# Down-projection of a decoder layer in two seven-product groups of eight blocks instead of one

## The chip, the cores and the metric

The kernel runs as one program on one core of a Trainium2 chip. The metric is the device time of that core in microseconds, the median of several runs of the same program. A separate profiled execution gives the trace; its span runs from the first to the last instruction.

## What is computed

One decoder layer in float32, 1024 tokens by 1024 channels. The change touches its last part only, the feed-forward block with a causal depthwise convolution, and the residual and norm behind it:

```python
def conv_ffn(xn, w_up, conv_w, conv_b, w_down):
    u = xn @ w_up                                  # (1024, 5632)
    c = conv_b + sum(upad[:, j:j + S] * conv_w[j] for j in range(3))
    gate, val = jnp.split(c, 2, axis=-1)
    return (jax.nn.silu(gate) * val) @ w_down      # w_down: (2816, 1024)
...
    x = x + conv_ffn(xn, w_up[l], conv_w[l], conv_b[l], w_down[l])
return rmsnorm(x, norm_final_w)
```

## The kernel before

Everything lies transposed: channels on the 128 partitions, tokens along the free dimension, two halves `hf` of 512 tokens. The hidden activation h has 2816 rows, 22 blocks of 128 (`NF`); the output has 1024 rows, 8 blocks `m`. Each float32 operand is split into two parts of the type fp32r, a high part (a cast on ScalarE, written ACT in the profile) and a low part (source minus high part, a subtraction on VectorE, DVE), and a product of two blocks is three matmuls: high by high, high by low, low by high (`product`, lines 835 to 837, and `mms`, line 996). `split` (lines 755 and 756) and `split_pair` (L110 and L112) and `load_w` (L129 and L131) make the parts for activations and weights.

Where a two by two arrangement of blocks is multiplied by a two by two arrangement, the kernel can form seven products of sums of blocks instead of eight products of blocks. The up-projection (`hidden`) does so for all its blocks. It names the weight blocks A11, A12, A21, A22 and the activation blocks B11, B12, B21, B22, with sums S1 to S4 of weights and T1 to T4 of activations. `sum_pair` makes the sums of weights on GpSimd (POOL, lines 96 to 99), four additions of 512 columns for a pair of outputs.

The last step of `hidden` stores h block by block to DRAM (`hd`); `down` reads it back. `raw_h` loads one half block (256 KB, tile `hr`, nine buffers) on the queue of SyncE (SP), `parts_h` splits it into a tile `h`; those tiles come in turn from two pools, 19 (`HP`) and 9 (`HPB`) of them.

`down` before the change:

- Plain blocks 0 to 5 (`N1 = 6`): 16 pieces, each one output `m` and three blocks, both halves, in `self.pieces`; four outputs at a time (first 4 to 7, then 0 to 3). The result is added to x, which lies in `x3` and is loaded from DRAM in two DMAs of 2 MB. In the course of these pieces the last steps of the convolution are finished (`DEFER`), their results stored (`STORE`), and the splits of the blocks needed next are made (`preps`, `sums`).
- Blocks 6 to 13 as one group of seven products. Rows m and m + 4 of the output form a pair. First a loop over the four pairs does the two products with A11 and A12; then a second loop does the other five products of each pair in turn (S1, S2, S4, S3, A22). The results are added to x on DVE directly from PSUM (lines 1052 to 1072).
- Blocks 14 to 21 plainly: 8 outputs for the first half, then for the second half, 24 matmuls each, with the squares for the last norm behind each. The last two outputs of the second half are done in quarters of 256 tokens, so that the norm (`last_norm`: column sums L158, `rstd_cols` L165 and L167, `spread` L173, scaling L1143, output DMAs L1144) starts earlier.

`next_w` returns the next weights; `ahead` loads and splits them one step before they are used, from two buffers for each of the tiles `wh`, `wl`, `sh` and `sl`, three of `raw` and two of `rv`; with `deep`, the load from DRAM is another step ahead. PSUM has eight banks here, four named `d` and four named `y`.

The order of the instructions on each engine isn't that of the code: a scheduler at build time takes, on each engine, the instruction of the highest priority (normally the first in the code) among those that are ready by its own costs, and a tile whose buffer is still taken isn't ready.

## Time and profile before

| what | value |
|---|---|
| median of 3 runs | 1355.06 us (1354.48 to 1355.87) |
| profiled execution, its own time | 1356.2 us |
| span of the profiled execution | 1354.3 us |
| granted TensorE clock, mean | 0.996 |
| busy in the span | PE 99%, weight loads (PEld) 81%, DVE 75%, ACT 45%, POOL 36% |
| HBM traffic | 129.61 MB read, 48.76 MB written |

In the profile PE is TensorE, SP the queue of SyncE from which the loads are issued. A row of the timeline gives the start in us, the time it took, the engine, the line of the kernel, the operation, the tile written and the tiles read, the shape and the count; in square brackets stands the idle time of the engine ahead of it and who ended it. Times are counted from the start of the span.

### The profile page before, as it was taken

Reading aid. Unit: us, or ns where it says so; the run is one execution under the profiler, and the core shown is the slowest. Engines: PE = TensorE matmul, PEld = TensorE weight load, DVE = VectorE, ACT = ScalarE, POOL = GpSimd, SP = SyncE. Lnnn points to the kernel's source line nnn. Section 1 sums busy time; section 2 is a strip of 40 time slices with the busy share of each in tenths; the row PEclk is TensorE's granted clock in tenths of the full one; section 3 lists DMA queues with packets and bytes.
Section 4 is the critical chain, followed back from the end, with each engine's and each line's share of the span. In section 5 each row is a group of like instructions: output and inputs, shape, how many; then the busy total and the mean of one; then the engine's idle time right before and its main releaser. Section 6 shows DMA issues by size and latency. Waiting matters only on the chain.

```text
span 1354.3 us, 17160 instructions
## 1 busy us (share of the span) xinstructions
PE 1335.0 (99%) x6304; PEld 1103.6 (81%) x6304; DVE 1009.8 (75%) x1454; ACT 603.9 (45%) x942; POOL 483.1 (36%) x350
## 2 busy tenths in 40 slices
PE   7999999999999999999999999999999999999997
PEld 6888888888887777878888888888888888888886
DVE  8846775388898875355689888888888898986454
ACT  8422232376667664334444334433443345433343
POOL 0436651010102125741455565555555611231011
PEclk9999999999999999999999999999999999999999
DMA  6334443966554235334422222122212248651342
GB/s 255 140 113 164 143 156 114 272 174 175 156 133 144 77 116 219 117 119 136 166 82 88 71 91 94 62 79 93 93 63 83 92 141 311 215 177 64 94 134 85
DMA packets 62470, 179.50 MB, mean 133 GB/s; under 512 B 6833, under 2 KB 15153, under 8 KB 62385
## 3 DMA queue, kind: packets, MB, share of 16 engines
q1 hardware_dynamic: 50928, 160.98, 36.7%
q10 hardware_dynamic: 11456, 17.41, 3.5%
q8 instruction: 50, 0.82, 0.2%
q14 instruction: 36, 0.29, 0.1%
HBM read 129.61 MB, written 48.76 MB: 132 GB/s over the span
## 4 chain that ended last, share of the span: by engine, by line
PE 62%; DVE 17%; POOL 7%; issue 7%; DMA 4%; ACT 3%; POOLq 0%; DVEq 0%; SPq 0%; ACTq 0%
PE t L836 7%; PE t L837 7%; PE t L835 7%; POOL us L965 3%; PE y L996 3%; PE d L996 3%; PE sc L568 3%; PE g L150 2%; PE g L151 2%; DVE c L958 2%; PE g L152 2%; DVE wl L112 2%; DMA gr<-gd 2%; PE sc L151 2%; PE sc L152 2%
## 5 line engine op out<-in xcount | busy, mean ns | idle before, releaser
L970 ACT ACTIVATE c<-us,vecs 128x1024 f32<-128x1024 f32 x44 | 54.8, 1248 | 163.2 <-POOL us L965 160.0
L965 POOL TENSOR_TENSOR us<-us,rstd 128x1024 f32<-128x1024 f32 x42 | 100.7, 2414 | 52.8 <-DVE wl L131 34.3
L110 ACT CAST sh<-sf 128x1024 fp32r<-128x1024 f32 x62 | 64.9, 1051 | 106.2 <-POOL sf L97 61.8
L129 ACT CAST wh<-raw 128x1024 fp32r<-128x1024 f32 (+2 forms) x60 | 60.7, 1012 | 104.8 <-PE sc L151 33.1
L971 DVE SCALAR_TENSOR_TENSOR c<-us,vecs,c 128x1024 f32<-128x1024 f32 x44 | 67.1, 1527 | 51.9 <-ACT c L970 51.9
L131 DVE TENSOR_TENSOR wl<-raw,wh 128x1024 fp32r<-128x1024 f32 (+2 forms) x60 | 75.3, 1256 | 39.1 <-ACT wh L129 29.3
L96 POOL TENSOR_TENSOR sf<-rv 128x512 f32<-128x512 f32 x30 | 42.5, 1417 | 166.7 <-DMA rv<-in_w_up 73.2
L112 DVE TENSOR_TENSOR sl<-sf,sh 128x1024 fp32r<-128x1024 f32 x62 | 88.3, 1426 | 8.2 <-ACT sh L110 8.2
L167 POOL TENSOR_TENSOR rs<-ms,mhalf 128x8 f32<-128x8 f32 (+2 forms) x9 | 14.5, 1614 | 159.1 <-DVE ms L165 148.5
L150 PE MATMUL g<-xh,wh 128*128 128x512 f32 x176 | 70.7, 402 | 0.1
L152 PE MATMUL g<-xh,wl 128*128 128x512 f32 x176 | 70.4, 400 | 0.0
L151 PE MATMUL g<-xl,wh 128*128 128x512 f32 x176 | 70.4, 400 | 0.0
L98 POOL TENSOR_TENSOR sf<-raw,rv 128x512 f32<-128x512 f32 x30 | 41.6, 1386 | 59.9 <-DVE sl L112 59.9
L572 DVE CUSTOM_DVE_ANT_0 L<-sc,bias 128x128 f32<-128x128 f32 (+7 forms) x64 | 47.7, 752 | 17.4 <-PE sc L568 14.1
L551 POOL MEMSET aT<- 128x128 f32 x32 | 6.1, 204 | 152.0 <-PE t L597 101.6
L573 ACT ACTIVATE L<-L,sm 128x128 f32<-128x128 f32 (+7 forms) x64 | 49.6, 778 | 20.7 <-DVE sm L572 18.2
L97 POOL TENSOR_TENSOR sf<-sf,raw 128x512 f32<-128x512 f32 x31 | 58.0, 1870 | 1.6
L972 DVE SCALAR_TENSOR_TENSOR c<-us,vecs,c 128x1024 f32<-128x1024 f32 x44 | 56.2, 1279 | 0.6
L725 POOL TENSOR_TENSOR gr<-gr,rstd 128x1024 f32<-128x1024 f32 x16 | 39.4, 2467 | 41.4 <-DMA gr<-gd 41.2
L112 DVE TENSOR_TENSOR wl<-raw,wh 128x1024 fp32r<-128x1024 f32 (+1 forms) x35 | 52.8, 1508 | 0.1
L151 PE MATMUL sc<-ml,wh 128*128 128x512 f32 x128 | 50.1, 391 | 0.6 <-DVE ml L746 0.6
L568 PE MATMUL sc<-u,u 128*128 128x512 f32 (+2 forms) x192 | 49.8, 359 | 0.1
(444 smaller groups left out, 4351.4 us busy)
## 6 DMA issues: line engine op xcount, KB each, us to landing
u<-qd SPq DMA_DIRECT2D x72, 256.0 KB, 6.1
raw<-in_w_down SPq DMA_DIRECT2D x27, 512.0 KB, 3.7
raw<-in_w_in SPq DMA_DIRECT2D x25, 512.0 KB, 4.4
hr<-hd SPq DMA_DIRECT2D x50, 256.0 KB, 5.3
raw<-in_w_up SPq DMA_DIRECT2D x23, 512.0 KB, 3.6
hd<-c SPq DMA_DIRECT2D x22, 512.0 KB, 2.8
rv<-in_w_up SPq DMA_DIRECT2D x21, 512.0 KB, 3.5
gr<-gd SPq DMA_DIRECT2D x16, 512.0 KB, 3.6
```

The source lines that it names most:

```text
L112: nc.vector.tensor_tensor(lo, src, hi.bitcast(F32), ALU.subtract)
L131: self.lo = (eng or nc.vector).tensor_tensor(wl, raw, wh.bitcast(F32), ALU.subtract)
L150: nc.tensor.matmul(ps, wh[:, kc + o, :], ah, start=first and n == 0, stop=False)
L151: nc.tensor.matmul(ps, wh[:, kc + o, :], al, start=False, stop=False)
L152: nc.tensor.matmul(ps, wl[:, kc + o, :], ah, start=False, stop=last and n == len(kcs) - 1)
L568: nc.tensor.matmul(sc[:, lo + n0:lo + n1], qs, k[c][part][:, n0:n1], start=part == 0, stop=part == 1)
L835: nc.tensor.matmul(ps, ah[:, k, :], bh, start=first and n == 0, stop=False, skip_group_check=skip)
L836: nc.tensor.matmul(ps, ah[:, k, :], bl, start=False, stop=False, skip_group_check=skip)
L837: nc.tensor.matmul(ps, al[:, k, :], bh, start=False, stop=last and n == len(ks) - 1, skip_group_check=skip)
L965: i = (nc.vector if m % NF == 0 else nc.gpsimd).tensor_tensor(us[:, 2:], us[:, 2:], self.rstd, ALU.mult)
L971: nc.vector.scalar_tensor_tensor(c, us[:, 1:T + 1], cw[1], c, ALU.mult, ALU.add)
L996: nc.tensor.matmul(ps, v[:, n, :], x, start=n == i == 0, stop=n == len(js) - 1 and i == 2)
```

## The change

The plain blocks at the front are three (`N1 = 3`), then come two groups of eight blocks (`NS = 8`) in seven products, then three plain blocks. Each group runs in three loops over the four output pairs: first A11 and A12; then S1, S2 and, one pair later, S4; then S3 and, one pair later, A22. Products of one pair are accumulated in the same PSUM bank and added to x in between: S4 upon S1, S2 upon the A11 product, S3 upon that, A22 upon that. So each of the seven products is followed by one addition of its bank to x, seven for a pair, where before there were nine.

The sums of weights are no longer made four at a time from one load: for the second loop (`"p2"`) the pair is loaded and three additions on POOL give S1, S2 and S4; for the third (`"p3"`) half of it is loaded again and one subtraction gives S3. Differences of h are made in two units, `sums_h2` (T1, T2 and the split of B22; one subtraction on POOL and one on DVE) and `sums_h3` (T3 and T4; two on POOL and one on DVE), where before `sums_h` made five on DVE; the halves of h are loaded for both. All preparations are one list `units`, of which each step takes a written number (`ready`). x is loaded in four DMAs of 1 MB. The weights of the last three blocks are split once and kept in h tiles (`last_w`), where before they were loaded twice. `HPB` is 7, `STORE` (1, 7), `DEFER` (2, 5).

```diff
-HP, HPB, HR = 19, 9, 9
-STORE = (1,9)
-DEFER = (4,8)
-N1 = 6
+HP, HPB, HR = 19, 7, 9
+STORE = (1, 7)
+DEFER = (2, 5)
+N1, NS = 3, 8
...
+    def sums_w(self, src, kind):
+        nc = self.nc
+        tt = nc.gpsimd.tensor_tensor
+        n = 2 if kind == "p2" else 1
+        g = self.tl(self.wp, [P, n, 4, P], "raw", bufs=RAW)
+        nc.sync.dma_start(g.rearrange("p a k c -> p (a k) c"), src[0][:, :4 * n])
+        v = self.tl(self.uw, [P, 2, 4, P], "rv", bufs=2)
+        nc.sync.dma_start(v.rearrange("p a k c -> p (a k) c"), src[1])
+        if n == 1:
+            tt(v[:, 0], g[:, 0], v[:, 0], ALU.subtract)
+            return (v, ("S3", "A22")), None
+        s = self.tl(self.cpl, [P, 2, 4, P], "c")
+        tt(s[:, 0], v[:, 0], v[:, 1], ALU.add)
+        tt(s[:, 1], s[:, 0], g[:, 0], ALU.subtract)
+        tt(g[:, 1], g[:, 1], s[:, 1], ALU.subtract)
+        return (s, ("S1", "S2")), (g[:, 1:2], ("S4",))
+
+    def split_sums(self, two, one):
+        ops = {}
+        for pool, h, l, part in ((self.uw, "sh", "sl", two), (self.wp, "wh", "wl", one)):
+            if part:
+                src, names = part
+                n = len(names)
+                hi, lo = self.split(*(self.tl(pool, [P, n, 4, P], t, F32R) for t in (h, l)), src)
+                for i, name in enumerate(names):
+                    ops[name] = hi[:, i], lo[:, i]
+        return ops
...
+        self.pieces = [4, 5, 6, 7, 0, 1, 2, 3]
+        src += [(self.w_dn[m:m + 2, :, :N1, :].rearrange("m p k c -> p m k c"), 2 * N1) for m in self.pieces[::2]]
+        for a in (N1, N1 + NS):
+            for kind in ("p1", "p2", "p3"):
+                for m in range(4):
+                    g, v = (self.w_dn[o, :, a:a + NS, :] for o in (m, m + 4))
+                    src.append((g, NS) if kind == "p1" else ((g, v), kind))
...
-    def sums_h(self, k):
-        b11, b12, b22, b21 = (self.raw_h(N1 + j, hf) for j, hf in ((k, 0), (k, 1), (k + 4, 1), (k + 4, 0)))
-        tt = self.nc.vector.tensor_tensor
...
+    def sums_h2(self, a, k):
+        b11, b12, b22 = (self.raw_h(a + j, hf) for j, hf in ((k, 0), (k, 1), (k + 4, 1)))
+        self.nc.gpsimd.tensor_tensor(b11, b12, b11, ALU.subtract)
+        self.nc.vector.tensor_tensor(b12, b22, b11, ALU.subtract)
+        for name, t in (("T1", b11), ("T2", b12), ("B22", b22)):
+            self.B[name, k] = self.parts_h(t)
+
+    def sums_h3(self, a, k):
+        b11, b12, b21, b22 = (self.raw_h(a + j, hf) for j, hf in ((k, 0), (k, 1), (k + 4, 0), (k + 4, 1)))
+        tt = self.nc.gpsimd.tensor_tensor
         tt(b12, b22, b12, ALU.subtract)
+        tt(b21, b21, b11, ALU.subtract)
+        self.nc.vector.tensor_tensor(b21, b21, b12, ALU.subtract)
+        for name, t in (("T3", b12), ("T4", b21)):
+            self.B[name, k] = self.parts_h(t)
...
+            units, self.lw = [], {}
+            for a in (N1, N1 + NS):
+                units += [lambda a=a, k=k, n=n, o=o: self.one_h(n, a, k, k + o, 0) for n, o in (("B11", 0), ("B21", 4)) for k in range(4)]
+                units += [lambda a=a, k=k, f=f: f(a, k) for f in (self.sums_h2, self.sums_h3) for k in range(4)]
+            units += [lambda j=j, hf=hf: self.load_h(j, hf) for hf in range(2) for j in range(N1 + 2 * NS, NF)]
+            units += [lambda m=m: self.last_w(m) for m in range(KC)]
...
+            ready = ((1, 1, 1, 1, 1, 2, 3, 3, 3, 1, 1, 0), (1, 1, 1, 1, 1, 2, 2, 2, 2, 2, 2, 2))
+            for g, counts in enumerate(ready):
+                counts, ys, late = list(counts), [], []
+                for m in range(4):
+                    wh, wl = self.next_w()
+                    y, ps = bank(1), bank(0) if g else pss[m, 0]
+                    ys.append(y)
+                    self.product(y, (wh[:, 0:4], wl[:, 0:4]), "B11", skip=True)
+                    self.product(ps, (wh[:, 4:8], wl[:, 4:8]), "B21", first=g > 0)
+                    for p in (y, ps):
+                        add(m, 0, p)
+                    prepare(counts.pop(0))
+                def p2(m, w, ps):
+                    self.product(ps, w["S4"], "B22", first=False, skip=True)
+                    add(m, 1, ps)
+                def p3(m, w, y):
+                    self.product(y, w["A22"], "T4", first=False, skip=True)
+                    add(m + 4, 0, y)
+                for m, y in enumerate(ys):
+                    w = self.next_w()
+                    ps = bank(0)
+                    self.product(ps, w["S1"], "T1", skip=True)
+                    add(m + 4, 1, ps)
+                    self.product(y, w["S2"], "T2", first=False, skip=True)
+                    add(m, 1, y)
+                    late.append((m, w, ps))
+                    if m:
+                        p2(*late.pop(0))
+                    if m == 3:
+                        p2(*late.pop(0))
+                    prepare(counts.pop(0))
+                for m, y in enumerate(ys):
+                    w = self.next_w()
+                    self.product(y, w["S3"], "T3", first=False, skip=True)
+                    add(m + 4, 1, y)
+                    late.append((m, w, y))
+                    if m:
+                        p3(*late.pop(0))
+                    if m == 3:
+                        p3(*late.pop(0))
+                    prepare(counts.pop(0))
...
-                    w = self.next_w()
+                    w = self.lw[m]
...
-                    mms(ps, w, 1, js, a, b, lambda n, m=m: tail.pop(0)() if a and n == (4 if m < KC - 1 else 2) else None)
+                    mms(ps, w, 1, js, a, b, lambda n, m=m: tail.pop(0)() if a and n == (1 if m < KC - 1 else 0) else None)
```

## The prediction

> **What bounds the kernel now.** I read the page first, for who is busy; then the chain of waits that ended last, for where the end comes from in the stage that changes; then the busy time by windows, for what the helpers have left there; then the timeline, for single durations.

> ```profile
> span 1354.3 us, 17160 instructions
> PE 1335.0 (99%) x6304; PEld 1103.6 (81%) x6304; DVE 1009.8 (75%) x1454; ACT 603.9 (45%) x942; POOL 483.1 (36%) x350
> ```

> PE has work in 99% of the span. So a matmul less is time less, as long as its operands are ready. The chain (columns: start, us, what) shows the stage to be a row of matmuls:

> ```profile
> 1111.23 2.04 PE d L1023 x9
> ...
> 1259.49 5.44 PE y L996 x24
> ...
> 1303.01 0.79 PE d L158 x8
> ...
> 1309.40 0.44 PE d L173 x4
> 1309.84 0.44 PE y L173 x4
> ...
> 1332.08 2.87 PE d L996 x24
> ...
> 1339.63 0.79 PE d L158 x8
> ...
> 1342.67 0.22 PE d L173 x2
> ...
> 1344.94 0.43 DVE x L1083
> ...
> 1345.87 0.84 PE d L158 x6
> ...
> 1346.97 0.70 POOL rs L167
> ```

> The down-projection begins at 1111.23 and its last matmul ends at 1344.94: 233.7 us, with 9.4 us behind it. One matmul of 512 columns costs 5.44 / 24 = 0.2267 us, one of 256 columns 2.87 / 24 = 0.12. What the stage's PE work should take, counted from the code: 288 (six plain blocks: 8 outputs x 2 halves x 6 x 3) + 336 (seven products x 4 pairs x 4 x 3) + 336 (eight plain blocks, less the last two outputs' second half) = 960 of 0.2267, 96 short ones of 0.12, and the sums and spreads (0.79 + 0.88 + 0.79 + 0.44): 217.6 + 11.5 + 2.9 = 232.0. PE stalls are only 1.7 us.

> The windows (busy us of PE, PEld, DVE, ACT, POOL; PE clock; DMA share; GB/s):

> ```profile
> 800.00:900.00 100.00, 99.81 (x437) 81.24 (x436) 86.26 (x84) 37.93 (x41) 57.64 (x43) 1.00 0.24 79
> ...
> 1110.00:1120.00 10.00, 10.00 (x46) 8.29 (x45) 8.50 (x12) 4.40 (x6) 1.62 (x1) 1.00 1.04 401
> ...
> 1150.00:1160.00 10.00, 10.00 (x45) 8.28 (x45) 9.97 (x13) 2.03 (x2) 0.66 (x1) 1.00 0.60 200
> 1160.00:1170.00 10.00, 10.00 (x45) 8.26 (x44) 9.06 (x11) 6.06 (x10) 6.25 (x4) 1.00 0.65 225
> ```

> PE is full in all four; DVE is nearly full too around 1150. DVE, with POOL beside it, is the next limit, and the change hands both more work per matmul.

> **What PE loses.** Plain blocks at the front 3 (144 matmuls), two groups (672), plain blocks at the end 3 (144): 960 instead of 1008. Of these 942 are long and 36 short: 213.6 + 4.3 + 2.9 = 220.8 us, which is 11.2 less than 232.0. This is certain; the question is how many stalls come in.

> **What DVE and POOL gain.** Prices come from these rows (start, us, what):

> ```profile
> 1114.73 0.95 DVE L131 TENSOR_TENSOR wl<-raw,wh 128x768 fp32r<-128x768 f32 x1
> ...
> 1118.53 3.09 DVE L756 TENSOR_TENSOR h<-hr,h 128x512 fp32r<-128x512 f32 x5
> ...
> 1129.97 2.38 POOL L965 TENSOR_TENSOR us<-us,rstd 128x1024 f32<-128x1024 f32 x1 [18.36 <-DVE wl L131]
> ...
> 1163.00 2.99 DVE L756 TENSOR_TENSOR h<-hr,h 128x512 fp32r<-128x512 f32 x3
> 1163.67 1.77 POOL L96 TENSOR_TENSOR c<-sl 128x512 f32<-128x512 f32 x1 [13.01 <-DMA sl<-in_w_down]
> ...
> 1165.92 0.67 DVE L1042 TENSOR_TENSOR x<-x,y 128x512 f32<-128x512 f32 x1
> 1166.51 2.88 DVE L756 TENSOR_TENSOR h<-hr,h 128x512 fp32r<-128x512 f32 x2
> ...
> 1168.92 1.62 POOL L99 TENSOR_TENSOR c<-raw,c 128x512 f32<-128x512 f32 x1
> 1169.96 1.67 DVE L112 TENSOR_TENSOR sl<-c,sh 128x1024 fp32r<-128x1024 f32 x1 [0.57 <-ACT sh L110]
> ...
> 1207.36 1.22 DVE L112 TENSOR_TENSOR sl<-c,sh 128x1024 fp32r<-128x1024 f32 x1
> ...
> 1208.70 1.29 POOL L96 TENSOR_TENSOR c<-raw 128x512 f32<-128x512 f32 x1 [6.62 <-DVE sl L112]
> ```

> Five splits in a row take 3.09, so a 512-column DVE operation costs 0.60, one of 1024 columns 1.20, one of 768 0.87. A POOL addition alone costs 1.29. Together they are dearer: from 1163.00 to 1171.63 DVE does five splits, one addition from PSUM and one split of 1024 columns, 4.8 us by those prices, waits 0.57 for ACT, and needs 8.63: 3.3 us are lost while POOL does four additions (5.2 us alone). Burst price: a POOL microsecond takes 63% of a microsecond from DVE. The addition from PSUM (L1042) took its plain 0.67 in the middle of it; the splits wait.

> [...]

> Stretch I runs from 1118.5, where DVE is done with the stage before, to the third phase of the first group. PE's part: plain blocks end at 1111.2 + 144 x 0.2267 = 1143.9, first phase 96 matmuls (21.8), second 144 (32.6): 1198.3, so 79.8 us. DVE in it: 28 splits of h (16.8) and 8 differences (4.8); weight splits 2 x 0.87 + 4 x 1.2 + 4 x 1.8 + 1.2 = 14.9; the last convolution steps, five operations of 1024 (6.0); 32 additions from PSUM (12 + 8 + 12; 19.2). Sum 61.7, of it 42.5 with both inputs in SBUF. POOL: 4 + 8 differences of h, 12 + 1 sums of weights, 25 x 1.29 = 32.3, and two L965 of 2.38: 37.0. Stretch II, from there to the third phase of the second group (21.8 + 21.8 + 32.6 = 76.2 us): DVE 16.8 + 4.8 + 16.8 + 28 additions (16.8) = 55.2, POOL 28 x 1.29 = 36.1. DVE and POOL together are 124% and 120% of the time. What such a load does to PE is shown by the up-projection before it, groups in 800 to 895.2 us (five steps of 84 matmuls; columns: line, operation, count, busy us, mean ns, idle):

> ```profile
> L971 DVE SCALAR_TENSOR_TENSOR c<-us,vecs,c 128x1024 f32<-128x1024 f32 x10 | 15.0, 1499 | 12.9 <-ACT c L970 12.9
> L112 DVE TENSOR_TENSOR sl<-sf,sh 128x1024 fp32r<-128x1024 f32 x10 | 12.1, 1212 | 0.0
> ...
> L396 DVE TENSOR_TENSOR us<-t,s 128x512 f32<-128x512 f32 x5 | 3.4, 684 | 0.0
> ...
> L112 DVE TENSOR_TENSOR wl<-rv,wh 128x512 fp32r<-128x512 f32 x5 | 3.4, 679 | 0.0
> ...
> L965 POOL TENSOR_TENSOR us<-us,rstd 128x1024 f32<-128x1024 f32 x10 | 24.3, 2451 | 0.7 <-DVE us L401 0.2
> ...
> L96 POOL TENSOR_TENSOR sf<-rv 128x512 f32<-128x512 f32 x5 | 6.5, 1294 | 26.8 <-DMA rv<-in_w_up 16.0 <-DVE c L972 10.8
> ```

> With the forms between them this is 40 operations of 1024 and 5 of 512 on SBUF (51), seven lines from PSUM x5 (21), and on POOL 20 additions and ten L965 (49.6): 121.6 in 95.2 us, 128%. There PE was busy 99.81 of 100. DVE's 86.26% are 82.1 us for 72 us of work, so a POOL microsecond cost DVE only 20%, and DVE still had 14% idle.

> Stalls from both sides. Low, priced as the up-projection: I (61.7 + 0.20 x 37.0) / 0.863 = 80.1, 0.3 late; II 72.3, not late. High, burst price and DVE idle 5% as in 1150 to 1170: I (61.7 + 23.3) / 0.95 = 89.5, 9.7 late; II (55.2 + 22.7) / 0.95 = 82.0, 5.8 late. So 0.3 to 15.5 us. By load the stage is nearer to the up-projection, but its PSUM additions come singly and not seven at a time, so fewer fall into POOL's shadow: I take 5, below the middle. [...]

> **Smaller edits.** The end: a piece is now 9 matmuls (2.04 us) instead of 24. The sums of squares need, on the last quarter, 0.93 us after their matmul (1344.94 to 1345.87); for a 512-wide piece twice that and one more DVE sum, 2.5, which 2.04 no longer cover: 0.4 late. In the quarters six short matmuls (0.72) now cover 0.93, and as many cover the 0.7 of L167 and its hand-overs: 0.2 each. Together 0.8 (0 to 2). The pieces of x, moved from two DMAs of 2 MB to four of 1 MB, the 28 more h tiles and the weights fetched twice: in I some 20 MB in 79.8 us, 250 GB/s, where 1110 to 1120 moved 401; hidden, and if that cover fails it shows as lateness inside the stall term. The last piece of x is issued on SP behind the store of the last hidden tile, which waits for DVE's product L958; by the sums of stretch I that is done before 1140, and the first reader of that piece comes with the first phase, at 1146.6. ACT is half idle. Two h buffers less (26 for 28): the 27th tile, T3 of the fourth block, waits for the first phase, which ends 32 us before its use: nothing. No price below zero is left out: nothing added can gain.

> **Sum.** 1111.2 + 220.8 + 5 + 0.8 + 9.4 = 1347.2 for the span, 7.1 less. The profiled execution took 1356.2 us, 1.1 above the median of 1355.06; from the median: 1348.0. (A run here can tell about 0.2%, 2.7 us, from no change.)

> **Rivals.** *The port becomes the bound.* At the burst price stalls are 15.5: 1358.5, and with 9% idle, between the two rows, I 13.6 and II 9.4 late: 1366. It ends slower than no change from stalls of 12.1 on, slower by 0.2% from 14.8. For it: 9.97 of 10 and 9.06 of 10 just where the change begins. Against it: the 99.81 at 128%. Chance 0.22, of it 0.04 within 0.2%.

> *Slots of the third phase.* S3 and A22 of a pair share one tile of two buffers, and A22 is multiplied one pair late. So the split for the third and the fourth pair can start only when A22 of the first and second is done.

> ```profile
> 9.89 0.74 PE L276 MATMUL t<-xh,wh 128*128 128x512 f32 x2
> 10.69 0.50 PE L277 MATMUL t<-xl,wh 128*128 128x512 f32 x1
> ...
> 1204.50 1.06 ACT L110 CAST sh<-c 128x1024 fp32r<-128x1024 f32 x1 [4.28 <-PE y L836]
> ...
> 1205.56 1.27 DVE L1061 TENSOR_TENSOR x<-x,d 128x512 f32<-128x512 f32 x2
> 1206.76 0.68 DVE L1063 TENSOR_TENSOR x<-x,y 128x512 f32<-128x512 f32 x1
> ```

> Before, such a split waits for PE in the same way (1204.50). In the new order PE would stand for 1.06 + 1.22 less two matmuls, 1.83 us, four times: 7.3 more, 1355.3. While ACT stands for such a slot, the splits of h behind it on ACT, and those of DVE that need them, stand too. Against it: the queues aren't in the written order. The split at 1207.36 is written ahead of L1061 and L1063 and runs behind them, and PE, written as L276, L277, L278, ran two L276 together. So A22 of the second pair, whose 2.72 us are ready, can be put ahead. [...] Chance 0.11, 0.01 of it slower.

> *Nothing is late.* Stalls 0.3: 1343.3. Chance 0.13.

> **The numbers.** Forecast 1348.0, stalls 2 to 9: 0.54. Faster by over 0.2%: 0.54 + 0.13 = 0.67; within: 0.10 + 0.04 = 0.14; slower: 0.18 + 0.01 = 0.19. The range runs from 1343.0, nothing late, to 1361.0, which leaves out the upper part of the port case, some 0.13.

> **What would show it.** Right: 78 matmul instructions fewer on PE's row of the page (6226), 0.2267 for each, last matmul 10 to 4 us earlier, idle PE in the second phases released by DVE splits. Port: DVE over 95% busy from 1150 to 1300, POOL additions at 1.7, PE waiting for splits in both groups. Slots: PE waiting twice in each third phase for ACT `sh` and DVE `sl` behind L836 of A22. The forecast falls if PE idles over 9 us in the stage.

## The result, and the profile after

The changed kernel takes 1387.75 us (median of 4 runs, 1385.23 to 1390.01) against 1355.46 us for the kernel before on the same chip (4 runs, 1354.48 to 1356.83). The ratio is 1.0235, with a 95% interval of 1.0223 to 1.0248: 2.3% slower, where 1348.0 us and a range to 1361.0 had been forecast. The profiled execution of the changed kernel took 1385.23 us.

The page of the changed kernel, its first rows:

```profile
span 1383.4 us, 17210 instructions
PE 1337.6 (97%) x6226; PEld 1099.8 (79%) x6226; DVE 1047.5 (76%) x1490; ACT 610.9 (44%) x958; POOL 543.2 (39%) x390
```

The 78 matmuls are gone (6226 for 6304), and yet PE's busy time is larger than before (1337.6 for 1335.0) and its share of the span smaller. Both are seen in the busy time by windows of the changed kernel (columns: busy us of PE, PEld, DVE, ACT, POOL; PE clock; DMA share; GB/s):

```profile
800.00:900.00 100.00, 99.50 (x434) 80.70 (x433) 86.26 (x82) 38.06 (x41) 56.79 (x41) 1.00 0.24 81
...
1144.00:1260.00 116.00, 90.28 (x343) 70.48 (x344) 94.72 (x106) 40.66 (x61) 63.60 (x42) 0.90 0.72 240
...
1230.20:1237.00 6.80, 5.62 (x13) 4.51 (x14) 4.16 (x7) 0.55 (x2) 1.68 (x2) 0.50 0.99 357
...
1254.10:1257.50 3.40, 2.96 (x7) 2.38 (x8) 2.75 (x4) 0.62 (x1) 2.08 (x2) 0.50 1.01 302
1257.50:1260.90 3.40, 3.40 (x16) 2.79 (x16) 3.40 (x3) 2.29 (x4) 3.21 (x3) 1.00 0.90 294
...
1278.00:1300.00 22.00, 22.00 (x98) 18.21 (x97) 18.56 (x22) 6.69 (x9) 8.03 (x6) 1.00 0.27 89
```

The kernel before, in the same 116 us of its own span:

```profile
1144.00:1260.00 116.00, 115.24 (x507) 94.80 (x506) 91.49 (x116) 40.68 (x57) 26.89 (x17) 1.00 0.47 156
```

The up-projection (first row) runs as before. From 1144 to 1260 PE does 343 matmuls where it did 507, and in five stretches, of which two are shown, the granted clock is one half: 7 matmuls in 3.4 us and then 16 in the next 3.4. In the last row PE is full again.

What PE waits for, in the summed waits of the changed kernel from 1140 to 1260 (columns: us in total, times, longest), and below it what DVE waits for:

```profile
PE y L860 <- DVE x L1057: 9.7, 2, 4.9
PE y L862 <- DVE wl L157: 8.7, 4, 3.5
PE d L862 <- DVE sl L781: 3.2, 1, 3.2
PE d L860 <- ACT sh L780: 2.6, 1, 2.6
PE d L860 <- DVE x L1057: 1.8, 1, 1.8
...
DVE hr L982 <- POOL hr L980: 11.8, 3, 4.9
DVE x L1057 <- PE y L862: 4.9, 3, 2.6
DVE hr L972 <- POOL hr L971: 3.6, 2, 2.0
```

PE waits for DVE, and DVE waits for POOL, 15.4 us in all (L982 and L972). The chain that ended last shows how the one becomes the other; around the longest stall it does not touch PE at all:

```profile
1236.56 1.29 POOL hr L980
1237.85 5.17 issue
1243.06 1.29 POOL c L95
1244.44 2.15 POOL c L96
1246.64 1.15 issue
1247.79 1.29 POOL raw L97
1249.08 1.24 POOL hr L980
1250.35 1.73 DVE hr L982
1252.08 1.80 DVE h L781 x3
```

And the timeline of DVE there, with PE's first matmul behind the stall:

```profile
1243.40 2.03 DVE L781 TENSOR_TENSOR sl<-rv,sh 128x1024 fp32r<-128x1024 f32 x1 [0.22 <-ACT sh L780]
1250.35 1.73 DVE L982 TENSOR_TENSOR hr<-hr,hr 128x512 f32<-128x512 f32 x1 [4.91 <-POOL hr L980]
1252.00 1.88 DVE L781 TENSOR_TENSOR h<-hr,h 128x512 fp32r<-128x512 f32 x3
1253.81 1.27 DVE L1057 TENSOR_TENSOR x<-x,y 128x512 f32<-128x512 f32 x2
...
1254.54 0.79 PE L860 MATMUL y<-h,sh 128*128 128x512 f32 x1 [4.91 <-DVE x L1057]
```

PE had finished its bank at 1249.6. The addition that frees the bank (L1057) needs nothing but that bank, but it stands on DVE behind a difference (L982) that waits for POOL until 1250.35. That difference takes 1.73, beside an addition on POOL (L95, 1.26 from 1250.27), where with all sums on DVE the same line takes 0.70 in the mean; then three splits follow, and the addition runs at 1253.81. PE stands for 4.9 us, and starts again at half its clock (0.50 in the row from 1254.10).

The 5.17 us that the chain calls issue are, in POOL's timeline, a wait of 5.21 us for the load of a weight pair (`rv`). That load had stood on SP for 5.1 us until DVE had split the tile whose buffer it takes; that split came behind ACT's cast (`sh`), and the cast had waited 6.25 us for PE to be done with one of the two buffers of `sh`. So late matmuls make POOL late in turn.

**Where 29.1 us went** (span 1383.4 for 1354.3). The stage begins 1.1 earlier; PE's work is 11.2 less, as forecast. Stalls, counted wherever two matmuls start more than 0.6 us apart, each as that distance less 0.2267, sum to 28.7 where they were 0.8: 27.9 more. The matmuls begun at half clock, each counted as 0.2267 longer, cost 10.9 where there were none. From the last matmul's start to the end of the span it takes 11.4 instead of 9.7. That makes 28.2; the remaining 0.9 are delays too short to list. So about 39 us of stalls and lost clock stand where the prediction put 5.

By phases, 28.1 of the 28.7 us lie in the first group: 9.3 in its first phase, 8.1 in the second, 10.7 in the third, which takes from 1221.0 to 1258.1. The 336 matmuls of the second group run from there to 1334.9 without a stall, 76.8 us for 76.2 of work.

### The profile page after: what moved, and what is told of

It reads as the page before. It is cut to its first block, busy times and chain, and to the rows that moved or that the text cites. A ratio compares the mean times of both kernels' runs of the same rounds, so it can differ in the third digit from the quotient of the medians.

```text
span 1383.4 us, 17210 instructions
## 1 busy us (share of the span) xinstructions
PE 1337.6 (97%) x6226; PEld 1099.8 (79%) x6226; DVE 1047.5 (76%) x1490; ACT 610.9 (44%) x958; POOL 543.2 (39%) x390
## 4 chain that ended last, share of the span: by engine, by line
PE 69%; DVE 14%; issue 5%; DMA 5%; POOL 4%; ACT 2%; SPq 0%; POOLq 0%; ACTq 0%; DVEq 0%
PE t L862 9%; PE t L861 9%; PE t L860 9%; PE g L176 3%; PE g L177 3%; PE g L178 3%; PE sc L177 3%; PE sc L178 3%; PE sc L176 3%; PE sc L593 3%; DMA hr<-hd 2%; POOL us L1009 2%; DVE c L1002 2%; DVE wl L138 2%; DVE h L781 1%
## 5 line engine op out<-in xcount | busy, mean ns | idle before, releaser
L157 DVE TENSOR_TENSOR wl<-raw,wh 128x1024 fp32r<-128x1024 f32 (+1 forms) x43 | 55.7, 1297 | 35.5 <-ACT wh L155 25.8
L155 ACT CAST wh<-raw 128x1024 fp32r<-128x1024 f32 (+1 forms) x43 | 44.1, 1026 | 52.1 <-PE sc L177 33.2
L780 ACT CAST h<-hr 128x512 fp32r<-128x512 f32 x62 | 37.2, 620 | 64.8 <-POOL hr L980 16.6
L124 POOL TENSOR_TENSOR sf<-raw,rv 128x512 f32<-128x512 f32 x30 | 41.6, 1388 | 59.9 <-DVE sl L138 59.9
L781 DVE TENSOR_TENSOR h<-hr,h 128x512 fp32r<-128x512 f32 x62 | 59.3, 986 | 1.1 <-ACT h L780 1.0
L598 ACT ACTIVATE L<-L,sm 128x128 f32<-128x128 f32 (+7 forms) x64 | 49.6, 778 | 20.3 <-DVE sm L597 17.7
L750 POOL TENSOR_TENSOR gr<-gr,rstd 128x1024 f32<-128x1024 f32 x16 | 39.4, 2470 | 39.6 <-DMA gr<-gd 39.1
L138 DVE TENSOR_TENSOR wl<-raw,wh 128x1024 fp32r<-128x1024 f32 (+1 forms) x32 | 50.4, 1576 | 0.1
```

The costliest lines, as they stand in the source:

```text
L138: nc.vector.tensor_tensor(lo, src, hi.bitcast(F32), ALU.subtract)
L781: self.lo = (eng or self.nc.vector).tensor_tensor(lo, src, hi.bitcast(F32), ALU.subtract)
```

## The experiments

For each kernel three figures tell the most: stalls in the stage, counted as above, the loss at half clock, and the time from the last matmul's start to the end of the span. Before they are 0.8, 0 and 9.7; after the change 28.7, 10.9 and 11.4. The median of the kernel before was 1357.2 us on the chips of the first eight runs.

**What POOL computes, taken away by steps.** First, the 24 differences of h go from POOL to DVE; POOL keeps the sums of weights.

```diff
-        self.nc.gpsimd.tensor_tensor(b11, b12, b11, ALU.subtract)
+        self.nc.vector.tensor_tensor(b11, b12, b11, ALU.subtract)
...
-        tt = self.nc.gpsimd.tensor_tensor
+        tt = self.nc.vector.tensor_tensor
```

> The changed kernel with the 24 differences of h that it makes on POOL made on DVE. Port theory (POOL's reading additions and DVE's two-input operations shut one another out): each of the 24 cost DVE 0.63 x 1.29 = 0.8 us and now costs 0.6, so 5 us at most are won: 1380 to 1384. Queue theory (PE waits because one late hand-over, load to POOL to DVE, holds everything behind it in DVE's and SP's queues): 24 hand-overs go, for which DVE waited 15.4 us and POOL itself 30 us on h loads: 1365 to 1372.

Measured: 1373.99 us, ratio 1.0125 (1.0095 to 1.0154); 19.6, 6.8, 11.4. It lies between the two theories, so it decides neither, but it says that DVE with 24 more operations does better. From 1144 to 1260 DVE is busy 110.27 us of 116 and waits for POOL nowhere, since it makes all differences itself; 32 sums of weights are still on POOL. PE waits 12.8 us for additions that free its banks (L1057), against 11.5 in the changed kernel. At one such stall the addition stands on DVE behind operations that take 1.74 to 1.79 each, while POOL makes four sums (1234.02 to 1240.54):

```profile
1234.24 1.79 DVE L982 TENSOR_TENSOR hr<-hr,hr 128x512 f32<-128x512 f32 x1
1235.96 1.78 DVE L980 TENSOR_TENSOR hr<-hr,hr 128x512 f32<-128x512 f32 x1
1237.66 1.76 DVE L781 TENSOR_TENSOR h<-hr,h 128x512 fp32r<-128x512 f32 x1
1239.35 1.74 DVE L981 TENSOR_TENSOR hr<-hr,hr 128x512 f32<-128x512 f32 x1
...
1241.62 0.68 DVE L1057 TENSOR_TENSOR x<-x,y 128x512 f32<-128x512 f32 x1
...
1242.35 0.80 PE L860 MATMUL y<-h,sh 128*128 128x512 f32 x1 [3.94 <-DVE x L1057]
```

So such a stall comes about without any result that DVE fetches from POOL.

Second, POOL keeps its place, its inputs and about its time, but reads far less: of each difference of h the first 32 of 512 columns are computed, of each sum of weights 32 of every 128, and the rest of the time goes into two fills of the result. The other columns of the sums are left out.

```diff
+    def write_only(self, out, a, b, op):
+        g = self.nc.gpsimd
+        g.tensor_tensor(out[..., :32], a[..., :32], b[..., :32], op)
+        for _ in range(2):
+            g.memset(out, 0.5)
```

> Each of the 56 sums and differences on POOL in the down-projection computes its first 32 columns only, and two fills of the tile (no input) follow, so that POOL takes about as long but reads almost nothing; the values of the other columns are left out. Port theory: DVE's splits are no longer shut out, PE loses under 8 us instead of 37: below 1358. Queue theory: the hand-overs and POOL's time stay, so 1378 to 1388.

Measured: 1364.65 us, 1.006 (1.0037 to 1.0083); 10.8, 4.8, 11.1. Third, POOL's 56 operations are left out.

```diff
-        self.nc.gpsimd.tensor_tensor(b11, b12, b11, ALU.subtract)
...
-            tt(v[:, 0], g[:, 0], v[:, 0], ALU.subtract)
-        tt(s[:, 0], v[:, 0], v[:, 1], ALU.add)
-        tt(s[:, 1], s[:, 0], g[:, 0], ALU.subtract)
-        tt(g[:, 1], g[:, 1], s[:, 1], ALU.subtract)
```

> The 56 sums and differences on POOL in the down-projection are left out; the splits take the loaded tiles as they are. Both theories expect most of the 37 us of PE back: 1348 to 1356. What is left above 1347 is neither port nor POOL's place in the chain: loads that come late behind waiting issues on SP, the buffers, and the end.

Measured: 1355.14 us, 0.999 (0.9978 to 1.0002); 6.7, 0, 11.5. The same 116 us in the run with fills and in the run without POOL's sums:

```profile
1144.00:1260.00 116.00, 107.21 (x444) 85.01 (x443) 88.35 (x126) 50.78 (x76) 70.68 (x143) 0.96 0.83 278
```

```profile
1144.00:1260.00 116.00, 110.78 (x481) 89.08 (x480) 94.11 (x136) 50.92 (x75) 0.00 (x0) 1.00 0.82 282
```

With fills POOL is busier than in the changed kernel (70.68 for 63.60), and PE does 101 matmuls more. So POOL's load and its place in the queue are not the main thing; its reading is: 23.1 us of time between 1387.75 and 1364.65. The queue theory, which wanted 1378 to 1388 here, falls as the main cause. Another 9.5 us go with POOL's operations altogether; how much of them is the queue and how much the reading that is left, these two runs don't tell. In the run with fills DVE still waits 14.9 us for POOL's last fill ahead of one kind of difference, and 3.2 ahead of the other (L978), together more than the 15.4 of the changed kernel:

```profile
DVE hr L988 <- POOL hr L86: 14.9, 7, 3.9
```

How the two engines meet is seen in groups by line and form, 1144 to 1300. First the changed kernel, DVE's splits and two of POOL's lines; then the splits of the run with fills:

```profile
L781 DVE TENSOR_TENSOR h<-hr,h 128x512 fp32r<-128x512 f32 x54 | 51.2, 978 | 0.8 <-ACT h L780 0.7
L781 DVE TENSOR_TENSOR sl<-c,sh 128x1024 fp32r<-128x1024 f32 x8 | 14.0, 1747 | 2.7 <-ACT sh L780 2.7
L1057 DVE TENSOR_TENSOR x<-x,y 128x512 f32<-128x512 f32 x26 | 17.5, 677 | 7.0 <-PE y L862 6.9
...
L96 POOL TENSOR_TENSOR c<-c,raw 128x512 f32<-128x512 f32 x8 | 13.4, 1680 | 15.6 <-DMA raw<-in_w_down 12.8 <-DVE x L1057 2.6
L980 POOL TENSOR_TENSOR hr<-hr,hr 128x512 f32<-128x512 f32 x8 | 12.1, 1514 | 1.3 <-DMA hr<-hd 1.3
```

```profile
L787 DVE TENSOR_TENSOR h<-hr,h 128x512 fp32r<-128x512 f32 x54 | 35.9, 695 | 3.3 <-ACT h L786 3.2
```

The same 54 splits take 978 ns each beside POOL's readings and 695 beside its fills; the additions from PSUM take 677 in the midst of the readings. With POOL idle, in the run with all sums on DVE, the splits take 694 (x46, 1144 to 1260). So in these runs the splits, with both inputs in SBUF, are slowed beside POOL's readings (978) and not beside its fills (695), and the additions from PSUM are slowed by neither (677 and 680).

**A store out of the loads' way.** SP stands 17.2 us at the two stores of the last hidden tiles, 9.2 of them at the last one, with loads behind it; the last store goes to ACT's queue.

```diff
-        store = lambda c0=self.c0: nc.sync.dma_start(self.hd[j], c0)
+        store = lambda c0=self.c0: (nc.scalar if j == NF - 1 else nc.sync).dma_start(self.hd[j], c0)
```

> The store of the last hidden tile is issued on ACT's queue instead of SP's. In the changed kernel SP stood 9.2 us at it with loads of h behind. Queue theory: the first three PE gaps (2.5, 3.7 and 0.9 us, with a half clock behind the second) shrink: 1378 to 1383. Port theory: DVE is as full as before, 1385 to 1389.

Measured: 1384.82 us, 1.0204 (1.0175 to 1.0234); 24.4, 12.2, 11.4. Its interval overlaps that of the changed kernel; whether the wait costs anything isn't settled by it, but it is no large part.

**One group in the new order.** Plain blocks 0 to 5, one group of eight in three phases, eight plain blocks: as many matmuls as before, the form of the change, half its sums.

```diff
-N1, NS = 3, 8
+N1, NS = 6, 8
...
-            for a in (N1, N1 + NS):
+            for a in (N1,):
```

> One part of the change alone: the three phases with their POOL sums, but for one group only (blocks 6 to 13), with the six plain blocks ahead and the eight behind as before. PE has the same 1008 matmuls as the kernel before. If the form of the phases is what costs, the group loses as much as the first group of the changed kernel did (15 us of gaps and some 7 at half clock): 1370 to 1377. If it is the density of two groups in a row (124% and 120% for DVE and POOL together, with 33 us of plain blocks ahead instead of 65), one group with a long lead loses little: 1354 to 1361.

Measured: 1361.55 us, 1.0028 (1.0012 to 1.0044); 3.6, 0, 9.5. The three phases by themselves cost some 4 us. What is dear comes with the second group: its sums are made while the first is multiplied (42 of the 56 on POOL fall between 1144 and 1260), and the stalls lie in the first group. But this run also puts six plain blocks ahead of the group instead of three, and it doesn't tell the density from the shorter lead.

**POOL work that nobody waits for, in the kernel before.** In the seven later pieces and the four first-phase steps, 26 additions on a tile that isn't used then; in a second kernel, fills in the same places.

```diff
+    def extra(self, n):
+        g, r = self.nc.gpsimd, self.rstd
+        for _ in range(n):
+            g.tensor_tensor(r[:, :H2], r[:, H2:], r[:, :H2], ALU.add)
...
+                if i > 8:
+                    self.extra(2)
...
+                self.extra(3)
```

> The kernel before with 26 POOL additions of 512 columns that nobody waits for: two behind each of the last seven plain pieces, three behind each pair of the first loop (they work on the tile rstd, which is free there). The computation is unchanged. Port theory: 26 x 0.8 = 21 us of DVE are lost between 1150 and 1207, where it was 96% busy, so PE loses 10 to 25: 1365 to 1380. Queue theory: nobody waits for them, only the pair sums behind them on POOL can come later: 1355 to 1360.

```diff
-            g.tensor_tensor(r[:, :H2], r[:, H2:], r[:, :H2], ALU.add)
+            g.memset(r, 0.5)
+            g.memset(r[:, :128], 0.5)
```

> The same places and the same POOL time as in the run with 26 additions, but as fills, which read nothing. Port theory: 1355 to 1358, and the difference to the additions is the port. Queue theory: the same time as with the additions.

Measured: 1385.61 us, 1.021 (1.018 to 1.024), with additions (25.2, 5.0, 9.6); 1362.98 us, 1.0038 (1.0019 to 1.0058), with fills (4.6, 1.8, 9.7). Both are above what the port theory expected. For the run with additions the reason is in its timelines, here of POOL, DVE and PE:

```profile
1150.43 44.29 POOL L978 TENSOR_TENSOR rstd<-rstd 128x512 f32<-128x512 f32 x26
...
1174.95 8.57 DVE L756 TENSOR_TENSOR h<-hr,h 128x512 fp32r<-128x512 f32 x5
1183.44 0.68 DVE L1049 TENSOR_TENSOR x<-x,y 128x512 f32<-128x512 f32 x1
...
1201.80 0.80 PE L835 MATMUL y<-h,wh 128*128 128x512 f32 x1 [17.32 <-ACT wh L129]
```

26 additions in a row need 1.70 each, and five splits in a row 1.71 each: one for one. But 17.3 us of this run's stalls are one wait. The kernel's own sums stand on POOL behind all 26 additions, until 1194.7; ACT's cast of them (`sh`, L110), and behind it on ACT the cast of the next weights, wait with them. In the other kernel those sums came behind 15 of the fills, at 1170.9. So the difference of 22.6 us is not the contention alone: much of it is POOL's queue, in another order and of another length. The pair shows the price of one meeting, and not what the whole is worth; the run with fills in the changed kernel, where POOL's time did not shrink, is the cleaner one for that.

**All sums on DVE.** The 56 operations go from POOL to DVE, computed in full.

```diff
-        tt = nc.gpsimd.tensor_tensor
+        tt = nc.vector.tensor_tensor
...
-        self.nc.gpsimd.tensor_tensor(b11, b12, b11, ALU.subtract)
+        self.nc.vector.tensor_tensor(b11, b12, b11, ALU.subtract)
...
-        tt = self.nc.gpsimd.tensor_tensor
+        tt = self.nc.vector.tensor_tensor
```

> The changed kernel with all 56 sums and differences of the down-projection on DVE, none on POOL. Port theory: each operation costs DVE 0.6 instead of 0.8 or more, and the hand-overs go: below the 1374 of the version with 24 of them moved, 1362 to 1370. If DVE's plain amount of work is what counts, 33 us more of it end above 1374, up to 1385.

Measured: 1353.64 us, 0.9973 (0.9961 to 0.9984); 5.0, 0, 11.4. Better than expected, and faster than the kernel before. Its windows:

```profile
1144.00:1260.00 116.00, 112.20 (x489) 90.97 (x489) 114.65 (x175) 47.63 (x70) 0.00 (x0) 1.00 0.83 274
...
1200.00:1222.00 22.00, 22.00 (x98) 18.12 (x98) 21.48 (x33) 9.04 (x12) 0.00 (x0) 1.00 0.88 294
...
1278.00:1300.00 22.00, 21.65 (x94) 16.92 (x93) 13.70 (x21) 5.58 (x9) 0.00 (x0) 1.00 0.35 108
```

DVE is busy 114.65 of 116 us, against 94.72 in the changed kernel; PE gets 489 matmuls for 343. And the stretches around the third phases of both groups (last two rows) are full or nearly so: PE doesn't wait for the tiles of S3 and A22, and the first of these phases takes 21.8 us, where it took 37 in the changed kernel.

Once more, on another chip (median of the kernel before there 1356.64 us, 23 runs):

> The run with all sums and differences on DVE once more, with more rounds: theory (each pair of a POOL addition and a two-input DVE operation costs more time than DVE alone needs for both): 1352.5-1354.5 us, 2.5-4 us below the kernel before. A chance result of one round: within 1 us of the kernel before.

Measured: 1354.38 us, 0.9984 (0.9975 to 0.9993); 4.9, 0, 11.3. Faster than before in both, by 0.16 to 0.27%: a small gain, and of the size that a run here just tells from none.

**Is it the matmuls, or only POOL?** The kernel before, its sixteen sums of weights for the down-projection on DVE:

```diff
-        tt = nc.gpsimd.tensor_tensor
+        tt = (nc.vector if first else nc.gpsimd).tensor_tensor
```

> The kernel before with the sixteen sums of the down-projection's weight pairs on DVE instead of POOL. If all-on-DVE gains by having fewer matmuls: there is nothing to gain here, as PE's gaps in the stage are 0.8 us, and DVE gets 9.6 us more work where it is at 79%; 1355-1360 us. If it gains only by taking POOL away from DVE, whatever the products: 1352-1354 us.

Measured: 1355.17 us, 0.9991 (0.9983 to 1.0); no stalls, 9.6 at the end. Taking POOL's sums away brings the old products at most 0.17%. Between the two kernels with all these sums on DVE, 1354.38 and 1355.17, the intervals overlap: of the 11.2 us of matmuls saved, hardly anything arrives.

**The end.** The waits of the run with all sums on DVE show one of ACT's squares, `PE d L184 <- ACT sl L1140`, of 1.8 us at the very end; its timeline there:

```profile
1341.62 1.55 DVE L1197 TENSOR_TENSOR x<-x,d 128x512 f32<-128x512 f32 x2 [1.08 <-PE d L199]
1343.09 0.42 DVE L1137 TENSOR_TENSOR x<-x,y 128x256 f32<-128x256 f32 x1
```

The last addition of the last quarter (L1137) stands behind the scaling of the quarter before it (L1197). So the scaling is put behind that addition, and only its spread stays ahead:

```diff
                     sq = evac(ps, m, 1, a, b)
+                if a:
+                    tail.pop(0)()
...
         def rest():
-            spread()
             for i in range(len(pieces)):
...
-        return [sums, rest] if b - a < H2 else ...
+        return [sums, spread, rest] if b - a < H2 else ...
```

> All sums and differences of the down-projection on DVE, as in the run with all of them there (1353.64 us), and the end put in another order: behind the last matmul of the second half's last quarter, the scaling of the quarter before comes after the last addition on DVE, and no longer ahead of it (1.55 us of scaling stood ahead of that addition). Tail theory: the time from the last matmul's start to the end goes from 11.4 to 9.7-10.2 us, 1351.9-1352.5 us. If that scaling only moves into the last norm: no change, 1353-1354.5 us.

Measured: 1352.43 us, 0.9972 (0.9961 to 0.9984); 4.6, 1.8, 10.0. The end behaves as expected in the trace:

```profile
1340.83 0.69 DVE L1199 TENSOR_TENSOR x<-x,d 128x512 f32<-128x512 f32 x1 [1.08 <-PE d L199]
1341.43 0.41 DVE L1137 TENSOR_TENSOR x<-x,y 128x256 f32<-128x256 f32 x1
```

One scaling still runs ahead of the addition, the others behind it: 1.2 us less from the last matmul to the end than in the repeated run. In the median it is 1.95 us, with intervals that overlap. With the store on ACT's queue as well:

> The new end, and the second store of the hidden tile issued on ACT's queue instead of SP's. Wait theory (loads of hidden halves and weights stand behind that store on SP and are late for the first phase): the gaps of the first phase at 1150-1152 go, 1.5-2 us below the run with the new end alone, 1350-1351 us. If with POOL free of sums those loads are early enough: the same as the new end alone within 0.7 us.

Measured: 1352.39 us, 0.9969 (0.9958 to 0.9981); 6.3, 0, 10.6. The same as with the new end alone; the store's wait costs nothing there. These two are the fastest of all kernels run, 0.3% below the kernel before.

## Why the prediction was wrong

**PE's work** was right: 6226 matmuls, and with all sums on DVE the stage from the first to the last matmul's start takes 229.0 for 233.6 us. Of 11.2 us saved, 4.2 go into added stalls (5.0 for 0.8) and some 2.4 into delays too short to list; 4.6 remain, and the end takes 1.7 of them back.

**The stall term** is the step that failed: taken at 5 us, at most 15.5, it was 27.9 more than before, with 10.9 at half clock on top. Three things in it:

- *The price of POOL's reading was about right.* Against the run with all sums on DVE, the two-input forms of DVE from 1144 to 1260 took 22.8 us longer in the changed kernel (the sum over seven forms; the splits of h are 10.7 of them, the first row below for the changed kernel, the second for the run with all on DVE). POOL's 42 operations there are 54.2 us at 1.29: 42%, between the 20% of the up-projection and the 63% of the burst.

```profile
L781 DVE TENSOR_TENSOR h<-hr,h 128x512 fp32r<-128x512 f32 x43 | 39.4, 943 | 0.8 <-ACT h L780 0.7
```

```profile
L781 DVE TENSOR_TENSOR h<-hr,h 128x512 fp32r<-128x512 f32 x46 | 30.8, 694 | 0.0
```

- *The step from load to stalls was wrong.* The prediction added up DVE's work over a stretch and divided it by 0.86 or 0.95, as if PE waited only for work that doesn't fit. It took 5 of up to 15.5 because the additions from PSUM, coming singly, would fall less into POOL's shadow. They do take their plain 677 ns, but they stand in DVE's queue behind operations that are stretched or that wait, and PE waits 11.5 us for them. In the changed kernel DVE was busy 94.72 of 116, 82%, and waited 15.4 us for POOL in front of work that was ready. The change itself brought in these waits: a difference on DVE that needs one from POOL (L972, L982), ahead of the additions that free PE's banks. The prediction counted the operations and not this hand-over. With 42% and 0.82, its own formula gives 14.4 us late in stretch I ((61.7 + 15.5) / 0.82 = 94.2) and 9.6 in II ((55.2 + 15.2) / 0.82 = 85.8): 24.0, near to the 27.9 measured. But 0.82 comes from the run that it explains, and the formula fails beside it: with the 24 differences on DVE (95% busy) it gives 2.2 where stalls grew by 18.8, and with fills (76% busy, no price for reading) 1.4 where they grew by 10.0. And the prediction's proof, the up-projection at 128% with PE at 99.81, was of a stage with no less load: the changed kernel still has 56.79 us of POOL and 99.50 of PE in those 100 us. Load alone doesn't tell.
- *The clock was no term at all.* It had been 1.00 in all of the stage's windows before 1340, and in the changed kernel five of the seven stalls of over 2.2 us ended within 2 us of the start of a stretch at half clock: 10.9 us in all.

How much each is worth: making POOL's reads fills took 24.0 us off stalls and clock (39.6 to 15.6), leaving POOL's work out another 8.9 (to 6.7). How the contention and the hand-over share the cost stays open, as no run kept the one whole and took away only the other. Two come near. Without the hand-over, but with 32 of the 56 sums on POOL and 24 more operations on DVE, 26.4 of the 39.6 us are left; with the hand-over (18.1 us of DVE's waits), but with little reading, 15.6.

**The end** was 1.7 for 0.8, inside its 0 to 2, but not where it was put. It was neither the sums of squares nor the spread, but DVE's order there, as the run with the new end showed.

**Loads** were called hidden. With the sums on DVE the same loads leave 5.0 us of stalls, so they cost at most that there. In the changed kernel POOL waits 31.6 us for halves of h and 17.9 for weights from 1140 to 1260, and from 1144 on the chain passes through loads of h three times, about 5 us each. One load of weights, ahead of the longest stall, was late because its buffer was; how much of the rest comes from buffers that are freed late was not tried.

**The rivals.** In the prediction and the expectations the port is the name for the meeting of POOL's readings with DVE's operations; what the runs show of it is the price (978 ns a split for 695), and not what lies behind it. This rival was the right one, with 0.22, but its price of 1358.5 to 1366 was as short as the forecast's. Slots of the third phase: in part. In the changed kernel ACT waits 6.25 and 4.79 us for PE ahead of two casts of `sh` in the first third phase, which holds the two longest stalls; but in both PE waits for an addition and not for these tiles. With all sums on DVE the same two buffers leave that phase full, so alone they cost PE nothing. The second third phase is nearly full in both kernels. Nothing late: not in any kernel with this form.

**The signs** spoke clearly. PE idles far over 9 us; POOL's additions take 1.44 to 1.68 in the mean of a line. PE's waits, which the port theory wanted in both groups, came in the first only. And its sign of a DVE over 95% busy fails: 82% in the changed kernel, about 95% with the differences on DVE, 99% with all sums there.

## What to carry to other kernels

A sum that is moved from a nearly full engine to an idle one can be no relief: here 56 sums made the kernel 34 us slower on POOL than on DVE (1387.75 for 1353.64), where they cost no more than leaving them out (1355.14), with DVE at 99% busy and PE hardly waiting; beside POOL's readings DVE's splits took 978 ns each, beside its fills 695. Before moving work, look not only at busy shares but at who will wait for whom: here a difference on DVE that waited for POOL until 1250.35 held up work that was ready, an addition that frees a PSUM bank, from 1249.6 to 1253.81. And price a stall of TensorE with the clock that goes with it: here 10.9 us at half clock beside 28.7 of stalls.

## What the runs showed of the hardware

In the run with 26 additions in the kernel before, DVE's splits run one for one with POOL's additions: five in a row take 1.71 us each, where five take 0.62 each with POOL idle (3.09 from 1118.53 in the kernel before), and the additions take 1.70 each, where one alone takes 1.29. An addition from PSUM, behind those splits, takes 0.68.
